# Softmax over 4096 long rows: the narrow loads of the first tile at 512 columns in place of 1024

## The chip, the cores and the metric

One core of a Trainium2 chip runs the kernel alone. The metric is the device time of one execution in microseconds (us); the kernel before takes 2485.56 us, the median of three runs (2485.54 to 2485.92). VectorE is called DVE in the profile, ScalarE ACT, GpSimd POOL, and SP is SyncE, which here only issues DMAs. Data moves on the core's 16 DMA engines; "DMA engine" below means one of these 16.

## The reference

```python
batch, seq, vocab = 16, 256, 32768          # logits float32, temperature 1.0
scaled = logits / temperature
scaled = scaled - scaled.max(axis=-1, keepdims=True)
exp_scaled = np.exp(scaled)
return (exp_scaled / exp_scaled.sum(axis=-1, keepdims=True)).astype(np.float32)
```

A softmax over 4096 rows of 32768 numbers: 537 MB are read and 537 MB are written.

## The kernel before, in words

**Tiles.** Every row is cut into two halves of 16384 numbers (64 KB), so the input is a matrix of 8192 half rows that follow each other in memory at a distance of 64 KB. A tile is 128 half rows, one for each partition, 8 MB; there are 64 tiles, g = 0 to 63. Three tile buffers (`_BUFS`, L10) lie side by side in the tensor X, and tile g uses buffer g % 3. A tile is computed in place and stored from the buffer into which it was loaded.

**Compute of a tile.** It is cut into pieces of 6304, 5376 and 4704 columns (`_PLAIN`, L11; six smaller pieces in the last two tiles, `_LATE`, L12). DVE takes the negated maximum of each piece (L215), ACT takes the exponential of each piece and its sum (L275). Then small instructions exchange results between neighbouring partitions, which hold the halves of one row (L233 to L260), and each piece is scaled in place, some by DVE (L266), some by ACT (L294).

**Order of the DMAs.** All DMAs are issued by SP, in the order that `order` (L93) writes out: L0, L1, L2, S0, L3, S1, S2, L4, S3, L5, S4 and so on to L62, L63, S61, S62, S63 (L for a load, S for a store, with the tile's number). A store waits on SP for the scaling of its tile (L159, L163), a load for the store that frees its buffer (L144). As one engine issues them all, a waiting DMA holds back all later ones.

**The first tile's load.** `load_parts(0)` (L68) cuts tile 0 into a wide load, all 128 partitions and the columns up to 16384 - `_NARROW`, and the last `_NARROW` columns (L14). These last columns are not loaded with one DMA but with 19 narrow ones (L149), whose rows `narrow_rows` (L81) takes from the table `_NARROW_ROWS` (L15): 14, 13, 12, 11, 10, 9, 8, 7, 7, 6, 5, 4, 4, 4, 3, 3, 3, 3 and 2 rows, 128 in all, most rows first, and rows 9 apart within one DMA. Piece 0 and 1 of tile 0 need the wide load alone (`landed`, L198, waits only for the parts that overlap a piece); piece 2 starts at column 11680 and needs both. Tile 3 is loaded in two halves (L72), tile 0 stored in two, tile 63 in three; every other load and store is one DMA of 128 rows of 64 KB.

Of the kernel before, what the change touches and what calls it, by code (L numbers as in the profile page):

```python
# [10 lines left out]
_PLAIN = ((6304, 5376, 4704), (0,))  # L11
_LATE = ((4096, 3072, 3072, 2048, 2048, 2048), (3, 4, 5))  # L12
_LAST_STORES = ((0, 4096), (4096, 6144), (10240, 6144))
_NARROW = 1024  # L14
_NARROW_ROWS = (  # L15
    (13, 2), (12, 3), (14,), (11, 3), (10, 4), (9, 5), (8, 6), (7, 7), (4, 4, 3, 3),
)
# [330 lines left out]
```

## Time and profile before

| what | before |
|---|---|
| median of three runs | 2485.56 us |
| the profiled execution | 2485.45 us |
| its span in the profile | 2483.7 us |
| bytes read, written | 536.87 MB, 536.87 MB |
| mean rate over the span | 432 GB/s |
| DMA packets | 19267 |
| DVE busy, ACT busy | 1526.0 us, 1325.6 us |
| longest total wait of DVE | 617.4 us, for loads |
| longest total wait of ACT | 1045.6 us, for DVE's maxima |

The profiled execution's time is 1.75 us more than its span, which begins with the first and ends with the last thing that the profile records. Section 2 of the page cuts the span into 40 slices of 62 us and shows in tenths how busy each engine was; under it stand the mean busy share of the 16 DMA engines and the rate. A table by windows gives the same for stretches of one's choice; it counts a DMA packet in the window in which it starts. A packet is what a DMA engine moves in one go; here it is one row of one DMA, and a further packet of 4 bytes closes a DMA's share on each DMA engine and raises the semaphore. The trace keeps the start, the duration and the size of every packet, but not the DMA engine; in short stretches packets can be chained end to start, as sixteen lanes, each of which carries one DMA after the other.

### The profile page before, as it was taken

To read this page: it belongs to the slowest core of one execution; us is meant where nothing else is said; L and a number is where in the kernel's file an instruction comes from. 1 tells how busy PE (TensorE), PEld (TensorE's weight loads), DVE (VectorE), ACT (ScalarE), POOL (GpSimd) and SP (SyncE) were. 2 spreads that over 40 slices of the span, in tenths; PEclk is the share of its full clock that TensorE was granted. 3 is DMA by queue.
4 is the path that set the end of the run, shared out by engine and by line. 5 is a ranking of instruction groups with operands and counts; after the bars stand their busy time and mean duration, and the time that the engine had idled before them with its cause. 6 is when DMAs were issued, how large, how long until landed. Compare 5 with 4: busy or idle time off the path is not lost.

```text
span 2483.7 us, 1689 instructions
## 1 busy us (share of the span) xinstructions
DVE 1526.0 (61%) x776; ACT 1325.6 (53%) x529; POOL 0.2 (0%) x4
## 2 busy tenths in 40 slices
DVE  5845665666656656566565665656656666566665
ACT  4744645646546455464554645546455464554654
POOL 0000000000000000000000000000000000000000
DMA  9999999999999999999999999999999999999998
GB/s 409 432 437 431 432 437 434 434 433 437 433 432 437 434 434 434 435 434 433 436 434 434 434 435 435 433 435 435 432 435 435 436 432 435 436 432 435 435 436 387
DMA packets 19267, 1073.78 MB, mean 432 GB/s; under 512 B 2240, under 2 KB 2240, under 8 KB 2368
## 3 DMA queue, kind: packets, MB, share of 16 engines
q1 hardware_dynamic: 19264, 1073.75, 99.9%
q14 instruction: 3, 0.02, 0.0%
HBM read 536.87 MB, written 536.87 MB: 432 GB/s over the span
## 4 chain that ended last, share of the span: by engine, by line
DMA 61%; DVE 28%; ACT 7%; issue 2%; SPq 0%; DVEq 0%
DMA xs<-in_logits_dram 59%; DVE t L215 21%; ACT xs L275 6%; DVE xs L266 6%; DMA out_dram<-xs 3%; SPq L168 0%; ACT ee L286 0%; DVE junk L260 0%; DVE t L233 0%; DVE row L257 0%; ACT xs L294 0%; DVE row L237 0%; DVE junk L244 0%; DVEq L307 0%; DVEq L231 0%
## 5 line engine op out<-in xcount | busy, mean ns | idle before, releaser
L275 ACT ACTIVATE xs<-xs,t 128x6304 f32<-128x6304 f32 (+5 forms) x198 | 932.0, 4707 | 1052.5 <-DVE t L215 1045.6
L215 DVE TENSOR_REDUCE t<-xs 128x1 f32<-128x6304 f32 (+5 forms) x198 | 1110.0, 5662 | 617.4 <-DMA xs<-in_logits_dram 617.4
L294 ACT ACTIVATE xs<-xs,junk 128x6304 f32<-128x6304 f32 (+1 forms) x68 | 355.6, 5235 | 44.9 <-DVE junk L260 44.9
L266 DVE TENSOR_SCALAR xs<-xs,junk 128x5376 f32<-128x5376 f32 (+2 forms) x130 | 358.7, 2802 | 2.3
L233 DVE LOAD_MASK_SELECT t<-t x64 | 0.9, 14 | 282.8 <-ACT xs L275 282.8
L286 ACT ACTIVATE ee<-t,row 128x6 f32<-128x6 f32 (+1 forms) x64 | 19.2, 300 | 35.2 <-DVE row L237 35.2
L275 ACT ACTIVATION_READ_ACCUMULATOR xs<-xs,t 128x1 f32 x198 | 36.9, 186 | 0.0
L244 DVE CUSTOM_DVE_ANT_1 junk<-ee,t 128x6 f32<-128x6 f32 (+1 forms) x64 | 10.7, 166 | 23.5 <-ACT ee L286 23.5
L260 DVE TENSOR_SCALAR junk<-ee,row 128x3 f32<-128x3 f32 (+1 forms) x64 | 14.6, 228 | 2.2
L257 DVE RECIPROCAL row<-row 128x1 f32<-128x1 f32 x64 | 10.5, 163 | 2.2
L237 DVE TENSOR_REDUCE row<-t 128x1 f32<-128x6 f32 (+1 forms) x64 | 10.2, 159 | 2.2
L233 DVE STREAM_SHUFFLE t<-t 128x6 f32<-128x6 f32 (+1 forms) x64 | 10.4, 163 | 0.5
L244 DVE DVE_READ_ACCUMULATOR2_ANT row<- 128x1 f32 x64 | 5.3, 82 | 0.0
L275 ACT ACT_TABLE_LOAD x1 | 1.3, 1283 | 0.9 <-SPq L127 0.9
L329 POOL MEMSET const-bfloat16-1.0<- 128x1 bf16 x1 | 0.1, 101 | 0.0
L329 POOL MEMSET const-uint8-127<- 128x1 uint8 x1 | 0.1, 101 | 0.0
L329 POOL MEMSET const-float32-0.0<- 128x1 f32 x1 | 0.1, 98 | 0.2 <-issue 0.2
L329 POOL MEMSET const-float32-1.0<- 128x1 f32 x1 | 0.1, 98 | 0.0
## 6 DMA issues: line engine op xcount, KB each, us to landing
out_dram<-xs SPq DMA_DIRECT2D x2, 4096.0 KB, 28.0
xs<-in_logits_dram SPq DMA_DIRECT2D x2, 4096.0 KB, 19.3
xs<-in_logits_dram SPq DMA_DIRECT2D x1, 7680.0 KB, 21.1
out_dram<-xs SPq DMA_DIRECT2D x2, 3072.0 KB, 19.4
out_dram<-xs SPq DMA_DIRECT2D x1, 2048.0 KB, 12.2
xs<-in_logits_dram SPq DMA_DIRECT2D x62, 48.0
out_dram<-xs SPq DMA_DIRECT2D x62, 29.1
xs<-in_logits_dram SPq DMA_DIRECT2D x4, 12.0 KB
```

The costliest lines, as they stand in the source:

```text
L215: m = v.tensor_reduce(out=t[:, k : k + 1], in_=self.piece(k), axis=mybir.AxisListType.X, op=A.max, negate=True,)
L233: v.stream_shuffle(out=t[:, 2 * K : 4 * K], in_=t[:, 0 : 2 * K], mask=swap), "sh"
L237: v.tensor_reduce(out=r[:, 0:1], in_=tv[:, :, 0, :], axis=mybir.AxisListType.XY, op=A.min),
L244: v.tensor_tensor_reduce(out=f[:, 0 : 2 * K].rearrange("p (a k) -> p a k", a=2), in0=self.ev, in1=tv[:, :, 1, :], scale=1.0, scalar=0.0, o ...
L257: self.done(v.reciprocal(out=r[:, 2:3], in_=r[:, 1:2]), "rc")
L260: v.tensor_scalar_mul(out=f[:, 0:K], in0=e[:, 0:K], scalar1=r[:, 2:3]), "f"
L266: v.tensor_scalar_mul(out=xs, in0=xs, scalar1=f[:, k : k + 1]), k, self.p.own
L275: s = a.activation(out=xs, in_=xs, func=Exp, bias=t[:, k : k + 1], scale=inv_t, accum_out=t[:, K + k : K + k + 1],)
L286: a.activation(out=self.ev, in_=self.tv[:, :, 0, :], func=Exp, bias=r[:, 0:1], scale=-1.0),
L294: self.scaled(a.mul(out=xs, in_=xs, mul=f[:, k : k + 1]), k, self.p.on_act)
L329: nc = _bacc.Bacc("TRN2", target_bir_lowering=False, num_devices=1)
```

## The change

`_NARROW` becomes 512. The 19 narrow loads keep their rows and their order and are 512 columns (2 KB a row) wide in place of 1024 (4 KB); the wide load of tile 0 is 15872 columns (62 KB a row) wide in place of 15360 (60 KB). The count of DMAs, their order, the waits and every instruction of DVE and ACT stay as they are.

```diff
-_NARROW = 1024
+_NARROW = 512
 _NARROW_ROWS = (
     (13, 2), (12, 3), (14,), (11, 3), (10, 4), (9, 5), (8, 6), (7, 7), (4, 4, 3, 3),
 )
```

```python
def load_parts(g):
    if g == 0:
        return [(0, _W - _NARROW), (_W - _NARROW, _NARROW)]
```

## The prediction, made before the changed kernel ran

> **What bounds the kernel now.** I read the page's head and its section 2 first, then the timeline of the first 60 us, the windows at the end, and last the single packets.
>
> ```profile
> span 2483.7 us, 1689 instructions
> ...
> DVE 1526.0 (61%) x776; ACT 1325.6 (53%) x529; POOL 0.2 (0%) x4
> ...
> DMA  9999999999999999999999999999999999999998
> GB/s 409 432 437 431 432 437 434 434 433 437 433 432 437 434 434 434 435 434 433 436 434 434 434 435 435 433 435 435 432 435 435 436 432 435 436 432 435 435 436 387
> DMA packets 19267, 1073.78 MB, mean 432 GB/s; under 512 B 2240, under 2 KB 2240, under 8 KB 2368
> ...
> q1 hardware_dynamic: 19264, 1073.75, 99.9%
> ```
>
> DMA stands at 9 in 39 of 40 slices, DVE is busy 61% and ACT 53%. The bytes set the time. In the packets' records 15872 packets move 64 KB each, nearly all in 2418 ns (27.1 GB/s for one DMA engine; 16 make 434 GB/s, the rate of nearly every slice), one after the other without a pause. A DMA engine carries 1024 such rows: 1024 x 2.414 us between starts = 2472 us. What an edit can touch is the rest: 2485.45 - 2472 = 13 us.
>
> ```profile
> 0.95 0.38 SPq L151 DMA_DIRECT2D xs<-in_logits_dram  x1
> 1.38 13.88 SPq L149 DMA_DIRECT2D xs<-in_logits_dram  x19
> 15.31 0.89 SPq L151 DMA_DIRECT2D xs<-in_logits_dram  x2
> 22.10 17.34 DVE L215 TENSOR_REDUCE t<-xs 128x1 f32<-128x6304 f32 x3 [22.10 <-DMA xs<-in_logits_dram]
> ...
> 50.84 0.82 SPq L168 DMA_DIRECT2D out_dram<-xs  x2
> ```
>
> SP issues the 19 narrow loads in 13.9 us, and L1 at 15.3 us, before the wide load is through (its last closing packet is 19.6 us after the first packet, which starts at 1.96 us): the queue has work throughout. The end:
>
> ```profile
> 2470.00:2475.00 5.00, 0.00 (x0) 0.00 (x0) 0.00 (x0) 1.00 1.00 433
> 2475.00:2480.00 5.00, 0.00 (x0) 0.00 (x0) 0.00 (x0) 1.00 0.59 256
> 2480.00:2484.00 4.00, 0.00 (x0) 0.00 (x0) 0.00 (x0) 1.00 0.03 12
> ```
>
> Column 7 is the mean share of the 16 DMA engines (a packet counts where it starts). They stop one by one. The closing packets of the last store stand, counted from the first packet of the run, at 2474.84 us on the first DMA engine and 2479.995 on the last, mean 2476.56. **The last of 16 sets the end: 3.4 us after the mean**, 1.96 + 2479.995 = 2481.96, then 1.7 us to the end of the span and 1.75 us outside.
>
> **Where this spread comes from.** The page counts 2240 packets under 512 B. 132 DMAs of 128 rows close on 16 DMA engines each, 2112; the remaining 128 are one for each narrow row. So a narrow load of c rows uses c DMA engines, one row each, and not 16. (The Trainium skill, "DMA: Bandwidth & Descriptors", section on why a DMA increments its semaphore by 16, says that the largest count up to 16 that divides the rows is used, the lowest-numbered DMA engines first; the count of packets agrees.) Chaining the packets gives lanes with 19, 19, 18, 14, 11, 11 (one of these should be 10), 9 and so on down to 0, 0 narrow rows. So the narrow loads set the DMA engines off against each other: after L1 the 16 closing packets span 2.76 us. As the queue never runs dry, they keep this distance, and it grows where packets are held up: 3.07 us after L4, 3.47 after L5, 3.62 after L6, 3.94 after L7, 5.16 at the end.
>
> **The change part by part.**
>
> 1. Wide load: 8 rows a DMA engine, each 2 KB longer. 61440 B take 2267 ns and 65536 B 2418, so 4096 B cost 151 ns and 2048 B 75.5: **+0.60 us** on every DMA engine.
>
> 2. Narrow loads: n rows of 2 KB less. An undisturbed 4 KB packet takes 159 ns, that is 151 + 8; half width makes 75.5 + 8 = 84 by this line (no packet of 2 KB is in the trace; bounds 159, if the cost were fixed, and 79.5, if all of it went by bytes). With 84: **-75.5 ns x n**. Together +75.5 x (8 - n): n = 19: -0.83 us; 11: -0.23; 8: 0; 0: +0.60. The mean stays, as n is 8 in the mean. The distance after L1 becomes about 2.76 - 1.43 = 1.3 us.
>
> 3. Which DMA engine ends last? Followed lane by lane, the one at 2479.995 carried 11 narrow rows; those with 18 and 19 end at 2478.4 to 2478.9. The last owes its place to later hold-ups (it moved from 3.6 to 5.2 us behind the first one between L6 and the end), so of the shift only its own -0.23 reaches the end if the hold-ups stay: **-0.2 us**.
>
> 4. L0 to L1: in the records from 19.7 to 23.8 us every packet is slow, narrow ones up to 287 ns and the first of L1 3.3 to 3.8 us in place of 2.42: some 1.0 to 1.4 us lost on each DMA engine. This stretch ends where the last narrow row does (23.2). With half the bytes it could be half as long, -0.6 us; or the DMA engines begin L1 closer together and lose more (at the run's first packet all 16 start within 0.75 us and take 2.7 to 3.4 us in place of 2.27: up to +0.8 us). I take 0, between the two.
>
> 5. SP's 19 issues have the same shape but for the width: 13.88 us, 0; L1 behind them is issued 4 us before it is needed. DVE starts 0.6 us later, 22.7 us, and S0 is issued at 51.4; L1 and L2 keep the queue busy to 59.4 + 1.96 = 61.3, and a DMA starts about 1 us after its issue (0.95 to 1.96): cover 9 us. At the end S63 is issued at 2455.5, its first packet needed at 2457.4, 0.9 us to spare; its chain hangs on the last landing of L62, and a smaller spread adds to that.
>
> Sum: 2485.45 - 0.2 = **2485.2 us**; the median of the runs is 0.1 above the profiled execution, far inside the range.
>
> **A rule against it.** In the trace packets are slow where many DMA engines begin rows together (point 4). The Trainium skill, "DMA: Bandwidth & Descriptors", section "Latency and other measured facts", reports copies between HBM tensors whose rows lie at large powers of two apart at 103 to 207 GB/s, and supposes that streams in step meet in the same HBM channels. Here the rows lie 64 KB apart, a pitch it gives no number for; the trace's 434 GB/s shows none of it at a 2.8 to 5.2 us distance. By this rule a smaller distance brings losses back, which is the first rival.
>
> **Rivals.**
>
> *The DMA engines stand too close, and turns from loads to stores cost time (slower).* The shift of the mean closing time over the undisturbed 19.32 us is +0.09 us for L4, +0.07 for L5, +0.49 for L6, +0.04 for L7; from L8 on it is almost 0. It seems that hold-ups push the DMA engines apart until they no longer meet. If at half the distance no such order is found, each of some 60 turns costs the mean of these four, 0.17 us: 60 x 0.17 - 0.69 (already paid) = +9.7, 2494.9 us; with the mean of the two largest, 0.29, 2502; with the largest, 2514. It leaves the 0.2% from 0.09 us a turn on. Against it: the wide load, whose 16 DMA engines run within 0.62 us, has its last four rows at 2267 to 2319 ns, almost free; in the steady part the lanes' phases within a 2.41 us row include nine within 0.67 us, with packets of 2418. For it: stores in step are not in the trace.
>
> *The last DMA engine's hold-ups go.* With a smaller distance to start from, the end falls back to where the lanes with 18 and 19 rows stand: 2478.9 - 0.8 = 2478.1, 1.9 us less: 2483.6. With all in balance at the mean, 2482.0; with point 4's half as well, 2481.4.
>
> *The narrow loads don't get shorter.* If a 2 KB packet costs the 159 ns of a 4 KB one, there is only the wide load's +0.6: 2486.05, and the distance stays 2.76 us.
>
> **How the numbers follow.** 0.2% (5 us) is about what a measurement of this kernel can tell from no change. The forecast, within 1.2 us either way, gets 0.40; the fading of hold-ups (2482 to 2484) 0.15; unshortened narrow loads 0.10; the turns 0.33, the only case beyond 0.2% on the slow side; 0.02 for a gain over 5 us, for which even perfect balance (3.4) plus point 4 (0.6) falls short. So faster 0.02, same 0.65, slower 0.33. The range goes from 2483.0 (part of the fading) to 2502 (turns at 0.29 us): left out are some 0.06 below and 0.12 above. The forecast's own side, 2483.0 to 2486.4, holds 0.6.
>
> **What would show it.** 128 packets of 2 KB at about 84 ns, and a distance after L1 near 1.3 us, show points 1 and 2. DVE's first reduction at 22.7 us and no dip in the DMA row show point 5. The first rival shows as packets far over 2418 ns after 300 us and a rate below 434 in the middle slices. I am wrong if those slices fall to 430, or if the closing packets of the last store span as much as before with a higher mean.

## The result, and the profile after

| | before | 512 wide |
|---|---|---|
| runs | 20 | 20 |
| median | 2485.9 us | 2505.97 us |
| lowest, highest | 2485.08, 2486.27 | 2485.49, 2512.92 |
| profiled execution, span | 2485.45, 2483.7 | 2485.84, 2484.1 |

The changed kernel has no single time. Eight of its 20 runs lie at 2485.49 to 2486.90 us, where the kernel before lies; twelve lie at 2503.61 to 2512.92; none lies between. I call these the lower and the upper group. The ratio of the means is 1.0056 (95% interval 1.0039 to 1.0073); the ratio of the medians, 1.0081, says only that the upper group had the majority in these 20. In all comparisons below the kernel before was run beside the others, 106 runs with the first 20: each at 2484.80 to 2486.60 us, never in an upper group.

The profile that came with the result is of the lower group. A later profiled execution (e9, the same kernel, 2497.92 us) is of the upper one, so both can be laid beside the kernel before. The head of the page, first for the lower group, then for the upper:

```profile
span 2484.1 us, 1689 instructions
...
GB/s 412 439 428 436 435 426 435 438 433 430 437 436 427 439 436 432 432 438 436 426 439 437 435 428 438 436 426 439 437 436 427 438 435 428 438 437 436 427 439 384
...
q1 hardware_dynamic: 19264, 1073.75, 99.9%
```

```profile
span 2496.1 us, 1689 instructions
...
DMA  9999999999999999999999999999999999999998
GB/s 410 441 432 428 436 432 437 437 433 425 436 436 436 432 437 432 431 436 435 435 436 432 430 436 435 435 435 430 431 431 426 422 436 426 431 431 426 435 422 371
...
q1 hardware_dynamic: 19264, 1073.75, 99.8%
```

The bytes are the same, and the DMA row stands at 9 in both. A slice of 62 us holds 1.6 tiles, so single slices swing; the upper one's rate sinks from slice 28 on (1685 us), to 422 to 436. The loss comes late, and little of it is idle time: busy DMA engines move less. The start of the lower one's profile, to lay beside the same lines of before:

```profile
0.95 0.38 SPq L151 DMA_DIRECT2D xs<-in_logits_dram  x1
1.39 13.89 SPq L149 DMA_DIRECT2D xs<-in_logits_dram  x19
15.32 0.89 SPq L151 DMA_DIRECT2D xs<-in_logits_dram  x2
22.50 17.34 DVE L215 TENSOR_REDUCE t<-xs 128x1 f32<-128x6304 f32 x3 [22.50 <-DMA xs<-in_logits_dram]
```

SP's issues take the same time, and the first reduction begins 0.40 us later. The end, lower group and then upper group (a packet counts in the window in which it starts):

```profile
2470.00:2475.00 5.00, 0.00 (x0) 0.00 (x0) 0.00 (x0) 1.00 1.08 462
2475.00:2480.00 5.00, 0.00 (x0) 0.00 (x0) 0.00 (x0) 1.00 0.50 216
2480.00:2484.00 4.00, 0.00 (x0) 0.00 (x0) 0.00 (x0) 1.00 0.11 49
```

```profile
2480.00:2484.00 4.00, 0.00 (x0) 0.00 (x0) 0.00 (x0) 1.00 1.09 467
2484.00:2490.00 6.00, 0.00 (x0) 0.00 (x0) 0.00 (x0) 1.00 0.68 291
2490.00:2496.00 6.00, 0.00 (x0) 0.00 (x0) 0.00 (x0) 1.00 0.15 66
```

In the upper group all 16 DMA engines end later, not the last one alone. The closing packets of the last store have their mean at 2476.55 us before, 2476.64 in the lower profile, 2487.65 in the upper one, and the last of them 3.4, 3.7 and 5.0 us after the mean.

**What differs: the distance between the first and the last DMA engine.** From the packets' records, the time from the first to the last of the 16 closing packets of a load, in us (e1, e9 and e10 are further profiles of the changed kernel):

```
profile        L2    L4    L7    L13   L19   L25   L31   L43   L55   L62
before         2.76  3.07  3.94  3.96  3.98  3.98  3.98  4.27  4.74  4.98
512, result    2.42  3.04  4.10  5.42  5.97  5.97  5.97  5.97  5.97  6.02
512, e1        2.36  3.09  3.83  5.11  5.59  5.88  5.88  5.88  5.88  6.12
512, e10       2.35  2.74  3.64  3.87  4.32  4.32  4.32  4.32  4.65  4.91
512, e9 upper  2.35  3.24  4.14  5.49  6.21  6.55  6.55  7.80  8.46  8.65
256, e4 upper  2.96  2.99  4.54  5.59  6.89  8.45  9.06  9.06  8.62  7.73
```

In the lower profiles of this table the growth slows or stops somewhere between 4 and 6 us. In the upper ones it goes on to 8 us or more, e4 by tile 25, e9 after tile 43; there the slow rows begin. Of these two the one that comes to this point earlier, e4 at 2510.66 us, lost more.

**Why some 8.4 us is a limit.** A tile's period on each DMA engine is 16 rows of 2.414 us, 38.6 us. From the landing of a load on its last DMA engine DVE and ACT need 28.9 us until SP issues the tile's store (kernel before, timeline: the start of the reductions and the issue of that tile's store):

```profile
1863.45 17.34 DVE L215 TENSOR_REDUCE t<-xs 128x1 f32<-128x6304 f32 x3 [9.82 <-DMA xs<-in_logits_dram]
...
1892.33 0.33 SPq L168 DMA_DIRECT2D out_dram<-xs  x1
```

The first DMA engine wants that store 38.6 us after its own share of the load. Between stand the distance to the last one, some 0.5 us from landing to DVE's start (0.48 in the records of the kernel before), the 28.9, and up to 1 us from issue to first packet: 38.6 - 28.9 - 0.5 - 1 = 8.2 us is the spare time of the store. By the waits that the records show at the first DMA engine it is a little more: in e9 it stood still 0.27 us ahead of S47, whose own load L47 had a distance of 8.86, so 8.6. Beyond it the queue runs dry for the first ones.

**Where the loss sits.** Time of 64 KB rows beyond 2418 ns, in us for each DMA engine, added up over the turns from L4 to L61, by the time since the first DMA engine ended the load; the last column is the whole run:

```
profile          0 to 6   6 to 16   16 to 18   18 to 40   whole run
before           0.28     0.00      0.00       0.54       1.99
512, result      0.92     0.00      0.00       0.44       2.23
512, e9 upper    5.08     0.16      3.58       1.19       11.99
256, e4 upper    7.93     0.13      10.94      1.53       22.79
```

The difference to before, 10.0 us in e9 and 20.8 in e4, makes most of what the spans differ by (12.4 and 25.2). The rest, to 0.3 us, is a later last DMA engine (1.5 and 1.8) and more idle time than before (1.2 and 2.9; in e9 nearly all of it, 1.05, stands ahead of S63). In the first 6 us it is the late DMA engines, still on the last rows of the load, that take longer (rows of 2.5 to 3.6 us in e9 from L45 to L50) while the early ones store at 2418 ns. At 16 to 18 us it is the early ones, eight or more at once, on their last store row: in e9's S47 eight rows that start within 0.13 us take 3.16 to 3.48 us.

**What the slow last rows go by.** Standing still is not needed for them, and being in step is not enough. In e9's S45 no DMA engine waits, yet eight last rows take 2.86 to 3.18 us; the rows just before them, on DMA engines as near to each other, take 2418 ns. What does order them is the store's *lead*: the time from SP's issue of the store to the moment at which the first DMA engine has ended the load ahead of it and wants the store. For the stores S4 to S60 of all profiles but e8's (which has other rows), by lead; the loss is that of 64 KB rows starting at 16 to 18 us, for each DMA engine and turn:

```
lead, us       under 0.95   0.95-1.3   1.3-1.6   1.6-1.9   1.9-2.6   over 2.6
turns          46           45         23        48        21        558
loss, us       0.57         0.39       0.16      0.03      0.01      0.00
```

The four profiles with a lead under 1.9 us (e4, e5, e9, e12) follow the same steps each for itself; below some 0.95 us the first DMA engine also waits. The shortest lead of a profile is 4.4 us in the kernel before, 3.3 in the changed kernel's result, 2.8 with 2048 columns and 10.5 in e6. So a store that is issued too late costs time well before the queue runs dry. The loss in the first 6 us does not follow the lead so plainly.

### The profile page after: what moved, and what is told of

The parts are those of the page before. It is cut to its first block, busy times and chain, and to the rows that moved or that the text cites. A ratio compares the mean times of both kernels' runs of the same rounds, so it can differ in the third digit from the quotient of the medians.

```text
span 2484.1 us, 1689 instructions
## 1 busy us (share of the span) xinstructions
DVE 1526.2 (61%) x776; ACT 1325.6 (53%) x529; POOL 0.2 (0%) x4
## 4 chain that ended last, share of the span: by engine, by line
DMA 61%; DVE 28%; ACT 7%; issue 2%; SPq 0%; DVEq 0%
DMA xs<-in_logits_dram 59%; DVE t L215 21%; ACT xs L275 6%; DVE xs L266 6%; DMA out_dram<-xs 3%; SPq L168 0%; ACT ee L286 0%; DVE junk L260 0%; DVE t L233 0%; DVE row L257 0%; ACT xs L294 0%; DVE row L237 0%; DVE junk L244 0%; DVEq L307 0%; DVEq L231 0%
## 5 line engine op out<-in xcount | busy, mean ns | idle before, releaser
L257 DVE RECIPROCAL row<-row 128x1 f32<-128x1 f32 x64 | 10.5, 164 | 2.2
```

Source lines behind the costliest of these rows:

```text
L257: self.done(v.reciprocal(out=r[:, 2:3], in_=r[:, 1:2]), "rc")
```

## The experiments

Two theories went in after the result. *Distance*: DMA engines that start too close to each other fall into an order in which they collide at every turn from a load to a store. *Width*: the 2 KB rows, or the 62 KB rows, disturb by themselves. After the first four the distance theory was split: *first form*, the collisions alone cost the time, whatever compute does; *dry queue*, the cost begins where the distance passes the spare time of a store's issue.

**e1: the changed kernel again.**

> The changed kernel once more, unaltered. All theories: its times fall into two groups, near 2486 us and from 2503 to 2513 us, about half and half. If this profile falls into the upper group, distance theory (the 16 DMA engines start too close to each other and fall into an order in which they collide at the turns from loads to stores): some 22 us of packets over 2418 ns, spread over all loads of 64 rows, 0.3 to 0.4 us a tile. Width theory (the 2 KB rows or the 62 KB rows themselves disturb): the slow packets lie in tile 0 alone or right after it, and the middle slices are at 434 GB/s.

12 runs: nine at 2485.09 to 2486.01, three at 2499.72 to 2505.12. Ratio 1.0017 (1.0000 to 1.0034). The two groups are there again, in other shares. The profile fell into the lower one, so it didn't tell the theories apart.

**e2: narrow rows dealt out evenly.**

```diff
-_NARROW_ROWS = (
-    (13, 2), (12, 3), (14,), (11, 3), (10, 4), (9, 5), (8, 6), (7, 7), (4, 4, 3, 3),
-)
+_NARROW_ROWS = ((16,),) * 8
```

> Narrow columns 1024 wide as before, but the 19 narrow loads replaced by 8 of 16 rows each, so that every DMA engine carries 8 narrow rows and none is set off against another. Distance theory: the upper group in most or all runs, 2503 us or more. Width theory: as before, 2484 to 2486 us in every run (less than before where the end is more even, by up to 3.4 us).

11 runs: seven at 2486.84 to 2487.69, four at 2499.16 to 2506.54; ratio 1.0031 (1.0012 to 1.0049). Both missed. The upper group exists at 1024 columns, so the width theory falls; but it isn't "most or all", though the DMA engines stand only 0.74 us apart after L2. The profile (lower group) shows the distance growing by itself, from 0.74 after L2 to 5.07 after L19 and 5.48 after L25, where it stays.

**e3: half the distance at full width.**

```diff
-    (13, 2), (12, 3), (14,), (11, 3), (10, 4), (9, 5), (8, 6), (7, 7), (4, 4, 3, 3),
+    (16,), (16,), (16,), (16,), (13, 3), (12, 4), (10, 6), (9, 7),
```

> Narrow columns 1024 wide as before, but the rows dealt out so that the DMA engines carry 12 to 4 narrow rows in place of 19 to 0: 8 rows of 159 ns between first and last, 1.3 us, about the distance of the changed kernel, without its widths. Distance theory: two groups of times as in the changed kernel, or the upper one alone. Width theory: 2485 to 2486 us in every run.

12 runs: eleven at 2486.74 to 2487.80, one at 2504.66; ratio 1.0012 (1.0001 to 1.0024). Again an upper run at 1024 columns, against the width theory. Again fewer than a rule "the closer, the more often" would have.

**e4: 256 columns.**

```diff
-_NARROW = 1024
+_NARROW = 256
```

> The narrow loads 256 columns wide, with the rows of before: 19 rows of about 46 ns, 0.9 us between the DMA engines. Distance theory: the upper group at least as often as in the changed kernel. Width theory: the upper group more often still if narrower rows disturb more; it does not tell here, only that width and distance act together.

12 runs: five at 2485.75 to 2486.99, seven at 2497.65 to 2510.75; ratio 1.0046 (1.0022 to 1.0071). Its profile is of the upper group, and brought the dry-queue theory: the distance passes 8 us, the first DMA engine begins to wait ahead of stores, and the slow rows set in there; they are not there from tile 4 on.

**e5: slower compute, same DMAs.** The kernel before with

```diff
-_PLAIN = ((6304, 5376, 4704), (0,))
+_PLAIN = ((3072, 4096, 9216), (0,))
```

> The kernel before (narrow loads 1024 wide) with other pieces: 3072, 4096 and 9216 columns in place of 6304, 5376 and 4704, so that the last exponential begins later and is longer. By the rows of before (0.88 ns a column for the exponential, 0.52 for DVE's scaling) a tile's compute from landing to the store's issue grows from 28.9 to some 34 us, under the 38.6 us that its transfers take. The DMAs are the same. Dry-queue theory (the distance between the first and the last DMA engine may not pass the spare time of a store's issue, 8.3 us before and some 3.2 us here; beyond that the first ones run dry at each store, start again together and collide): every run in the upper group, 2500 us or more, from tile 5 or 6 on. Distance theory in its first form (the collisions at the turns alone cost the time, whatever compute does): 2486 us in every run.

Four runs, all at 2515.34 to 2523.15; ratio 1.0135 (1.0119 to 1.0150). Timeline:

```profile
1847.58 17.34 DVE L215 TENSOR_REDUCE t<-xs 128x1 f32<-128x3072 f32 x3 [4.84 <-DMA xs<-in_logits_dram]
...
1881.90 0.33 SPq L168 DMA_DIRECT2D out_dram<-xs  x1
1882.28 0.43 SPq L151 DMA_DIRECT2D xs<-in_logits_dram  x1
1886.42 17.34 DVE L215 TENSOR_REDUCE t<-xs 128x1 f32<-128x3072 f32 x3 [4.55 <-DMA xs<-in_logits_dram]
```

Compute takes 34.3 us (1881.90 - 1847.58), and DVE still waits 4.6 to 4.8 us for each load: compute isn't what fills the period. Yet the kernel before, which was never in the upper group, now loses 30 to 37 us in every run. The spare time by this chain is 8.2 - 5.4 = 2.8 us. Rows beyond 2418 ns cost 27.3 us for each DMA engine, 16.8 of them at 16 to 18 us. One thing was not as expected: the queue ran dry already at S2, where each DMA engine stands still for 4.6 us in the mean (the distance falls from 2.9 to 0.6 us there), before tile 5. The slow last rows are there in nearly every turn from S11 on, when the distance is back at 3.2 us. The first form of the distance theory falls.

**e6: less compute, same DMAs.** The changed kernel; the maximum and the scaling cover the first half of each piece alone, so half of both is left out (the second pair of lines stands twice, for DVE and for ACT):

```diff
-                    in_=self.piece(k),
+                    in_=self.piece(k)[:, 0 : self.p.pieces[k][1] // 2],
...
-                xs = self.piece(k)
+                xs = self.piece(k)[:, 0 : self.p.pieces[k][1] // 2]
```

> The changed kernel (512 wide) with shorter compute and the same DMAs: the maximum is taken over the first half of each piece and only the first half of each piece is scaled; this part of the work is left out. From landing to the store's issue some 23 us in place of 28.9, so that the spare time rises from 8.3 to some 14 us. Dry-queue theory: no run in the upper group; all 2485 to 2488 us. First form of the distance theory: two groups as in the changed kernel, a third to a half of the runs over 2500 us.

11 runs, all at 2485.02 to 2487.50; ratio 1.0004 (0.9995 to 1.0013). By the share of upper runs in the changed kernel (16 of 34, below) eleven lower ones in a row would have a chance of about 0.1%; by that of e1 alone (3 of 12) it is 4%, and on the chip of e5 to e8 the changed kernel itself was not run. Timeline:

```profile
1863.20 8.81 DVE L215 TENSOR_REDUCE t<-xs 128x1 f32<-128x3152 f32 x3 [16.04 <-DMA xs<-in_logits_dram]
...
1885.84 0.33 SPq L168 DMA_DIRECT2D out_dram<-xs  x1
```

22.6 us from start to issue; the spare time is 14.5 us. The distance grew to 5.2 us only and no run is in the upper group.

**e7: 2048 columns.**

```diff
-_NARROW = 1024
+_NARROW = 2048
```

> Narrow loads 2048 wide with the rows of before: the DMA engines start 19 rows of 311 ns apart, 5.5 to 6 us. First form of the distance theory (far apart is safe): about 2487.5 us in every run, the end later by 11 x 0.15 us. Dry-queue theory: the distance begins 2.5 us under the limit of 8.3 us, and hold-ups added 2.4 us in the kernel before and 3.5 us in the changed one; some or most runs over 2500 us.

11 runs, all at 2486.75 to 2487.27; ratio 1.0004 (0.9995 to 1.0013). Here the first form forecast right and the dry-queue theory's addition wrong: the distance starts at 5.94 us and grows to 6.52 only, not by another 2.4 to 3.5. It stays under the limit, so the limit itself is not touched; but what a start does to the growth can't be added from other kernels.

**e8: loads in halves, correct compute.** The changed kernel with

```diff
-    if g == 3:
+    if g >= 3:
         return [(0, _W // 2), (_W // 2, _W // 2)]
```

> The changed kernel with the loads of tile 3 and all later ones in two halves of 8192 columns, so that the maxima begin when the first half has landed. Rows of 32 KB (1213 ns, 4 to 9 ns more than half of 2418) cost 64 x 8 x 4 to 9 ns = 2 to 5 us. Dry-queue theory: the last landing is followed by half of the maxima only, the spare time rises by 7 us or more, and no run is in the upper group: 2487 to 2491 us in all. First form of the distance theory: two groups, some 22 us apart.

11 runs, all at 2490.52 to 2491.27; ratio 1.0020 (1.0011 to 1.0029). No upper group, as the dry-queue theory has it, at the price of shorter rows. In its profile the distance still grows, to 7.1 us, but no store has a lead under 9 us. A cure that computes everything, but dearer than the kernel before.

**e9 and e10: the changed kernel, two more single executions.**

> The changed kernel, unaltered, one profiled execution. Dry-queue theory: if it falls into the upper group (2497 us or more), the distance between the first and the last DMA engine grows past 8.3 us, and from that tile on, not before, the first DMA engine waits 0.2 to 1.3 us ahead of each store; if it falls into the lower group, the distance stays under 8.3 us to the end and no such wait occurs. First form of the distance theory: in the upper group the slow packets begin with tile 4 and the first DMA engine never waits.

> As e9: the changed kernel once more, one profiled execution, with the same expectation for either group.

e10, at 2485.00 us, stays at 4.3 to 5.0 us and never waits, as expected. e9, at 2497.92, passes 8 us after tile 43, and the slow rows begin there and not at tile 4: against the first form. But the waits are fewer than expected: three of over 60 ns (S47 0.27 us, S52 and S59 under 0.1). S45 and S49, with leads of 1.03 and 1.00 us, have the slow last rows with no wait at all. So the rows slow down when the store comes only just in time, and standing still is not needed. DVE's waits for loads in e9, 11.3 us more than the 617.4 of before, show the longer period:

```profile
DVE t L215 <- DMA xs<-in_logits_dram: 628.7, 60, 24.2
```

**e11: 768 columns.**

```diff
-_NARROW = 1024
+_NARROW = 768
```

> Narrow loads 768 wide: the DMA engines start 19 rows of 122 ns apart, 2.1 to 2.5 us, between the changed kernel and the one before. All that is settled so far (a larger distance at the start makes the growth stop earlier; over 8.3 us the queue runs dry): most runs at 2485.5 to 2487 us, a share of upper runs below that of the changed kernel (15 of 32), perhaps none. A share of half or more would speak against the distance at the start as what decides the growth.

12 runs: eleven at 2484.82 to 2486.68, one at 2509.11; ratio 1.0010 (0.9995 to 1.0025). As expected. The profile (lower group) comes to 6.8 us.

**e12: the limit set to between.** The kernel before with

```diff
+_SLOWER = ((4096, 4608, 7680), (0,))
...
-        widths, self.on_act = _LATE if g >= tiles - 2 else _PLAIN
+        widths, self.on_act = _LATE if g >= tiles - 2 else _SLOWER if g >= _HEAD else _PLAIN
```

> The kernel before (1024 wide) with pieces of 4096, 4608 and 7680 columns in tiles 4 to 61, and its own pieces in tiles 0 to 3. By the rows of e5 (0.865 ns a column for the exponential, 0.547 for DVE's scaling) a tile's compute from landing to the store's issue is some 32.8 us in place of 28.9, so that the spare time falls from 8.2 to some 4.3 us. The DMAs are the same, and the distance in the kernel before was 3.1 us at tile 4, 3.9 to 4.0 from tile 7 to 30, 4.3 at tile 43 and 5.1 at the end. Dry-queue theory: no wait of the first DMA engine ahead of its stores while the distance is under the spare time, waits from the tile on that passes it (near tile 43; earlier if the spare time is under 4.0), and a time between 2488 and 2515 us. If only the size of compute counted, and not the distance, the waits would begin at tile 4.

Four runs at 2514.11 to 2517.79, three of them over the 2515 expected; ratio 1.0122 (1.0105 to 1.0139). Timeline (the added line shifts the numbers by one):

```profile
1691.92 17.34 DVE L216 TENSOR_REDUCE t<-xs 128x1 f32<-128x4096 f32 x3 [6.23 <-DMA xs<-in_logits_dram]
...
1724.43 0.33 SPq L169 DMA_DIRECT2D out_dram<-xs  x1
```

32.5 us, so a spare time of 4.6. The waits begin neither at tile 4 nor near tile 43, but at S11. The distance was 3.1 us at L4, 3.7 at L6 and 4.3 at L7, over the 3.9 of the kernel before; at L9 (4.8) late DMA engines take 3.2 to 3.4 us for their last load rows, at S9 (lead 1.02 us) the slow last rows are there; L11 has 5.65, and ahead of S11 the first one waits 0.45 us. In later tiles the waits start at about 5.0 (S18 0.69 us with 5.72 for L18, S22 0.38 with 5.39 for L22), which is the 8.6 of e9 less the 3.6 us of longer compute. So the distance at which the waits start moves with compute, as the dry-queue theory has it. That the distance grows faster when little is to spare was not in it.

The runs together, upper ones of all: 2048 columns 0 of 11; 1024 0 of 106; 768 1 of 12; 512 16 of 34 (12 of 20, 3 of 12, 1 of 2); 256 7 of 12; 1024 evenly 4 of 11; 1024 at half the distance 1 of 12. No version tried beats the kernel before.

## Why the prediction was wrong

- **The time and the range.** Forecast 2485.2 us, range to 2502; the median is 2505.97, and the mean lies 0.56% above the kernel before. Two steps failed. In the sum it is point 5: it takes the queue as covered by the spare time of S0 and S63 alone, and so puts at nothing what stores in the middle of the run can lose by coming late; that was 10.0 us in slow rows in e9, and 20.8 us with 256 columns (e4). In the range it is the price of the first rival, which with a chance of 0.33 does name a loss at turns from loads to stores: "each of some 60 turns costs the mean of these four, 0.17 us", with 0.29 for the range's end. A turn in the loss costs some 0.6 us (e4's first DMA engine: 39.21 us a tile from L25 to L59, in place of 38.64), not all turns have it, and how many depends on when the distance reaches the limit.

- **Luck on both sides.** That the median is of the upper group is a draw of these 20 runs: the same kernel in e1 has a median of 2485.79. That there is an upper group is no draw. The forecast describes the lower group to 1 us (its median in the first 20 runs is 2486.1), but in part by luck, as points 2 and 4 missed and later hold-ups made up for it.

- **The rival's mechanism.** "It seems that hold-ups push the DMA engines apart until they no longer meet. If at half the distance no such order is found" had the right place and the wrong direction. The sign that the text names, slices down to 430, is there in e9 from 1685 us on. Hold-ups push the DMA engines apart, as it says, but that is no cure: where it doesn't stop, the stores of the first ones come too late, and rows slow down. e5 and e12 put a kernel that never had the loss into it with the same DMAs, in all eight runs; e6 and e8, where every store is issued 9 us or more ahead, had no upper run in 22.

- **Cover.** Point 5 looked for the spare time of S0 (9 us) and S63 (0.9 us), and left out all stores between, whose spare time is the 8.2 to 8.6 us that decide. The same sum for a tile in the middle, 38.6 - 28.9 - 0.5 - 1, needed only rows of the profile before, and would have shown a limit of 8 us beside a distance that had already grown from 2.8 to 5.2. The 0.9 us of S63 gave out too: in the result's profile six DMA engines wait 0.1 to 0.3 us ahead of it, in e9 nine wait 1.7 to 2.2 us; the text expected a smaller distance there, and it was larger (6.0 and 8.65 us after L62, 5.0 before).

- **Point 1** was right in sign: the first reduction came at 22.50 us, 0.40 later, where 0.60 was forecast (the wide load's last closing packet moved by 0.36 us).

- **Point 2**: the packet's price was right (84 ns for 2 KB, undisturbed), so the third rival falls. The distance was wrong: 2.40 to 2.70 us after L1 and 2.35 to 2.42 after L2, not 1.3. Beside the narrow rows there is what the DMA engines lose at the start of L1: in the result's profile those with 14 to 19 narrow rows take 3.18 to 3.26 us for their first row of L1, the ones with 0 to 6 take 2.93 to 2.97, while before it was the other way round (2.67 to 2.84 for the last four to begin, against 3.3 to 3.8; point 4 has the higher figure for all of them). What halved is the distance of the early ones: the first nine stand within 0.86 us after L2 before, within 0.32 to 0.56 in the profiles of the changed kernel.

- **Point 4** took 0 where it had named -0.6 us as possible. The mean of L1's closing packets came 0.71 us earlier, so the slow stretch did get shorter; later hold-ups took it back (the last mean is 0.08 us later than before).

- **Point 3** (which one ends last) doesn't matter beside this. The last closing packet is at 2480.39 us in the lower profile, 2480.00 before.

- **The rule against it.** What the Trainium skill supposes in "DMA: Bandwidth & Descriptors", section "Latency and other measured facts", for copies at larger distances between rows than the 64 KB here, that streams in step lose rate, would fit the run's first rows and the eight rows of S47 that started within 0.13 us (3.2 us each). But closeness alone is not enough: in the result's profile nine DMA engines stand within 0.33 us from L7 to L62, and their rows take 2418 ns. By that rule alone e2, with all 16 within 0.74 us, should have been the slowest; seven of its 11 runs were not.

**What stays open.** Why a run's growth stops at 4 to 7 us or doesn't: 512 and 256 columns have it in half of the runs, 1024 in none, and the two kernels with other deals of rows, which start closest, in 4 of 11 and 1 of 12, so the distance at the start alone doesn't order them. The shares are uneven for one kernel too (12 of 20, 3 of 12 and 1 of 2, in different series). How near to each other the early DMA engines stand could be it; no run here separates that from the number of narrow rows. And why a store with a short lead loses on its last row, 17 us after the early ones began it, and not on the first, is seen in every upper profile and not explained by one.

## What to carry to other kernels

A queue that is always full can still lose time: the DMA engines drift apart, and the distance between the first and the last is taken from the spare time of every transfer that waits for all of them. Work out that spare time for a tile in the middle of the run (period less compute from the last landing to the next issue) and set the growing distance beside it. Look at how long ahead of its need each transfer is issued, and not only for waits: here rows slowed from a lead of 1.6 us down, while waits began at 0.95. And a change of a few kilobytes at the start can cost nothing in one run and 23 us in the next, so take enough runs to see whether the times have one group or two.

## What the runs showed of the hardware

- Sixteen DMA engines that run without pause keep their distance for hundreds of microseconds to a few nanoseconds (before: 3982 ns from L25 to 3984 at L31), and add to it mostly where some still load while others store: late ones take up to 3.6 us for 64 KB then (e9, L45 to L50), the storing ones 2.418.
- The growth needs no start: DMA engines that began 0.74 us apart stood 5.5 us apart after 25 tiles (e2).
- A store issued less than some 1.6 us before the first DMA engine wants it makes that store's last rows slow, even where no DMA engine is idle: 0.16 us lost for each DMA engine at a lead of 1.3 to 1.6 us, 0.39 at 0.95 to 1.3, 0.00 in the 558 turns over 2.6.
- A small edit far from the end makes a kernel's time fall into two groups 14 to 20 us apart, on the same chip and in the same series of runs (e1: nine runs at 2485.09 to 2486.01, three at 2499.72 to 2505.12).
